# Rotary embedding on one core: unit 0's output is stored mostly from GpSimd's queue behind the loads, instead of from SyncE's beside them

## The chip, the cores and the metric

One core of a Trainium2 chip. The metric is the device time of one execution in microseconds (us). The profile's span is some 1.8 us shorter than that time.

## The reference

The input x is 8 x 8 x 1024 x 64 in float32 (16.78 MB), and the output has the same shape and type.

```python
angles = np.outer(positions * scale, freqs)          # scale = 0.5
cos, sin = np.cos(angles), np.sin(angles)
x_first, x_second = x[..., :half], x[..., half:]
out_first  = x_first * cos - x_second * sin
out_second = x_first * sin + x_second * cos
```

## The kernel before

The 64 heads are worked on in four units of 128 partitions x 8192 numbers, 4.19 MB each in float32. GpSimd's queue loads the units and casts them to float16 on the way. The first half of unit 0 comes this way too; its second half is staged in float32 through SyncE's and ScalarE's queues, in a buffer of the output pool. After a prologue that makes the tables of sines and cosines, VectorE (DVE in the profile) does four operations for each half unit. ScalarE (ACT) casts the half to float32 in an output buffer, and a DMA stores it.

```python
    xin = ctx.enter_context(tc.tile_pool(name="xin", bufs=1))
    xout = ctx.enter_context(tc.tile_pool(name="xout", bufs=3))   # staged half of unit 0, then OUT
    # ... (staged half, small tables)
    pin(nc.gpsimd.dma_start(out=Xf[0][:, :NH], in_=xv[0][:, :NH]))
    # ...
    for u in range(1, NU):
        pin(nc.gpsimd.dma_start(out=Xf[u], in_=xv[u]))
    # ... (tables of sin and cos into T)
    for u in range(NU):                       # NU = 4
        OUT = xout.tile([P, N], FP32, tag="O")        # N = 8192
        for s in range(2):
            # ... (ks, ns, Xs: the half; sin_b, cos_b: the tables, broadcast)
            pin(nc.vector.tensor_tensor(out=pr, in0=Xs, in1=sin_b, op=ALU.mult))
            pin(nc.vector.tensor_tensor(out=Xs, in0=Xs, in1=cos_b, op=ALU.mult))
            # ... (a subtraction and an addition, half as long)
            pin(nc.scalar.copy(out=OUT[:, ns], in_=Xf[u][:, ns]))
            if u in (0, NU - 1):
                pin(nc.sync.dma_start(out=ov[u][:, ns], in_=OUT[:, ns]))
        if u not in (0, NU - 1):
            pin(nc.gpsimd.dma_start(out=ov[u], in_=OUT))
```

Of the kernel before, what the change touches and what calls it, by code (L numbers as in the profile page):

```python
# [21 lines left out]
def kernel(  # L22
# [8 lines left out]
    nc = tc.nc  # L31
    pin = tc.keep_in_program_order
# [9 lines left out]
    NU = NBH // HEADS  # L42
# [2 lines left out]
    K8 = S // P  # L45
    G = P // HP
    W = K8 * half
    assert S % HP == 0 and D == 2 * half and NBH % HEADS == 0 and G * K8 == K

    fscale = float(scale)  # L50
# [2 lines left out]
    ov = out.rearrange("b h s d -> (b h s d)").rearrange("(u p n) -> u p n", p=P, n=N)  # L53
# [34 lines left out]
        out=one, in_=one, compare_op=ALU.not_equal, fill=1.0, base=0,  # L88
        pattern=[[-1, G], [-G, HP]], channel_multiplier=1,
    ))  # L90
    for u in range(1, NU):
# [9 lines left out]
        out=posf, in_=pos_i64.bitcast(I32).rearrange("p (k t) -> p k t", t=2)[:, :, 0]  # L101
# [3 lines left out]
        out=y,  # L105
# [8 lines left out]
        out=r, in0=m, scalar=_MAGIC, in1=y, op0=ALU.subtract, op1=ALU.subtract  # L114
# [5 lines left out]
        out=ra.bitcast(I32), in0=r.bitcast(I32), scalar1=0x7FFFFFFF, scalar2=None, op0=ALU.bitwise_and  # L120
# [5 lines left out]
    for g in range(0, G, 2):  # L126
        ps = spread.tile([P, 2, 2, W], FP32, tag="g")
        for i in range(2):
            nc.tensor.matmul(  # L129
                out=ps[:, i].rearrange("p t w -> p (t w)"),  # L130
# [9 lines left out]
    pin(nc.scalar.copy(out=Xf[0][:, NH:], in_=X0f[:, :NH]))  # L140


    for u in range(NU):
        OUT = xout.tile([P, N], FP32, tag="O")
        for s in range(2):
            ks = slice(s * KH, (s + 1) * KH)
            ns = slice(s * NH, (s + 1) * NH)
            Xs = X[u][:, ks]
            sin_b = T[:, 0, ks].unsqueeze(2).broadcast_to((P, KH, 2, half))
            cos_b = T[:, 1, ks].unsqueeze(2).broadcast_to((P, KH, 2, half))  # L150
            pr = tmp.tile([P, KH, 2, half], FP16, tag="pr")
            pin(nc.vector.tensor_tensor(out=pr, in0=Xs, in1=sin_b, op=ALU.mult))  # L152
            pin(nc.vector.tensor_tensor(out=Xs, in0=Xs, in1=cos_b, op=ALU.mult))  # L153
            pin(nc.vector.tensor_tensor(  # L154
                out=Xs[:, :, 0, :], in0=Xs[:, :, 0, :], in1=pr[:, :, 1, :], op=ALU.subtract
            ))
            pin(nc.vector.tensor_tensor(  # L157
                out=Xs[:, :, 1, :], in0=pr[:, :, 0, :], in1=Xs[:, :, 1, :], op=ALU.add
            ))
            pin(nc.scalar.copy(out=OUT[:, ns], in_=Xf[u][:, ns]))  # L160
            if u in (0, NU - 1):
                pin(nc.sync.dma_start(out=ov[u][:, ns], in_=OUT[:, ns]))
        if u not in (0, NU - 1):
            pin(nc.gpsimd.dma_start(out=ov[u], in_=OUT))  # L164
# [1 line left out]
_INS = ['x', 'freqs', 'positions', 'scale']  # L166
_OUTS = [((8, 8, 1024, 64), 'float32')]
# [30 lines left out]
```

## Time and profile before

| | us |
|---|---|
| time, median of 3 runs | 84.39 |
| span of the profile | 82.5 |
| engine total: shares of the DMA queues, summed, times the span | 80.0 |
| data of the last store ready | 73.2 |
| last store landed | 81.6 |

The profile gives each DMA queue's packet time as a share of the 16 engines' span. Their sum times the span is how long 16 engines need for all the bytes. By the bytes they carry, q0 in the profile is GpSimd's queue, q1 SyncE's and q10 ScalarE's. A "DMA" row cuts the span into 40 slices and gives the engines' busy share in tenths. The page's list of DMA issues of this kernel shows where bytes wait (KB are counted on the SBUF side, the last column is the median from issue to landing):

```profile
out_dram<-OUT SPq DMA_DIRECT2D x4, 2048.0 KB, 14.8
out_dram<-OUT POOLq DMA_DIRECT2D x2, 4096.0 KB, 15.3
X<-in_x_dram POOLq DMA_DIRECT2D x3, 2048.0 KB, 31.9
```

A transfer of 2.1 MB takes 14.8 us here. At the rate of the engines it would move in 4.9, so most of the time it stands in a queue or takes turns with another.

### The profile page before, as it was taken

How to read it: one execution, taken by the hardware profiler on the slowest of the kernel's cores; microseconds unless marked ns; L12 is line 12 of the kernel's file. 1: busy time of each engine (PE TensorE's matmuls, PEld its weight loads, DVE VectorE, ACT ScalarE, POOL GpSimd, SP SyncE). 2: the span in 40 equal slices, each digit the busy share in tenths (PEclk: the TensorE clock that was granted, in tenths of full speed). 3: DMA queues.
4: the chain of work that ended last, by engine and by line, in shares of the span. 5: the costliest groups of instructions: out<-in, count | busy, mean ns of one | idle time of the engine just before them, and what ended most of it. 6: DMA issues, size and time to landing. Idle time of an engine off the chain costs nothing.

```text
span 82.5 us, 179 instructions
## 1 busy us (share of the span) xinstructions
PE 7.1 (9%) x18; PEld 2.8 (3%) x18; DVE 60.3 (73%) x40; ACT 40.1 (49%) x18; POOL 4.6 (6%) x14
## 2 busy tenths in 40 slices
PE   0020999200000000000000000000000000000000
PEld 0020333000000000000000000000000000000000
DVE  0306476999999999999999999999999997000000
ACT  0603069999950790393098059219606902940000
POOL 4920000000000000000000200000200000000000
PEclk9999999985555555555555555555555555555555
DMA  2899998997996999799979999996998999799990
GB/s 48 336 319 278 290 326 187 254 246 159 230 254 127 254 262 342 270 278 350 278 191 302 270 342 421 461 524 286 508 509 350 413 508 461 302 445 429 397 485 24
DMA packets 1874, 26.22 MB, mean 318 GB/s; under 512 B 338, under 2 KB 338, under 8 KB 338
## 3 DMA queue, kind: packets, MB, share of 16 engines
q0 software_dynamic: 864, 15.73, 66.2%
q1 hardware_dynamic: 720, 9.44, 27.5%
q10 hardware_dynamic: 290, 1.06, 3.3%
HBM read 16.79 MB, written 16.78 MB: 407 GB/s over the span
## 4 chain that ended last, share of the span: by engine, by line
DVE 55%; ACT 15%; issue 6%; DMA 5%; PE 5%; DVEq 1%; ACTq 0%
DVE X L153 20%; DVE pr L152 20%; DVE X L157 9%; DVE X L154 6%; DMA freq_row<-in_freqs_dram 5%; ACT T L139 5%; ACT OUT L160 4%; PE ps L129 4%; ACT X L140 4%; DVEq L193 1%; PE cfreq L97 1%; ACT tab L122 1%; DVE r L113 1%; DVE y L104 1%; ACTq L69 0%
## 5 line engine op out<-in xcount | busy, mean ns | idle before, releaser
L160 ACT CAST OUT<-X 128x4096 f32<-128x4096 f16 x8 | 28.9, 3607 | 24.2 <-DVE X L157 24.2
L152 DVE TENSOR_TENSOR pr<-X,T 128x4096 f16<-128x4096 f16 x8 | 18.3, 2292 | 1.0 <-ACT T L139 0.7
L153 DVE TENSOR_TENSOR X<-X,T 128x4096 f16<-128x4096 f16 x8 | 18.3, 2292 | 0.3
L154 DVE TENSOR_TENSOR X<-X,pr 128x2048 f16<-128x2048 f16 x8 | 9.8, 1225 | 0.3
L157 DVE TENSOR_TENSOR X<-pr,X 128x2048 f16<-128x2048 f16 x8 | 9.7, 1218 | 0.0
L139 ACT CAST T<-ps 128x1024 f16<-128x1024 f32 x6 | 5.7, 1028 | 2.6 <-PE ps L129 2.6
L129 PE MATMUL ps<-tab,sel 128*128 128x512 f16 x16 | 6.5, 599 | 2.2 <-ACT tab L122 2.2
L164 POOL DMA_DIRECT2D out_dram<-OUT x2 | 1.1, 538 | 54.1 <-ACT OUT L160 54.1
L137 DVE CAST T<-ps 128x1024 f16<-128x1024 f32 x2 | 2.5, 1225 | 2.2 <-PE ps L129 2.2
L140 ACT CAST X<-X0f 128x4096 f16<-128x4096 f32 x1 | 3.6, 3649 | 0.0
L95 DVE COPY sel<-one 128x2048 f16<-128x2048 f16 x1 | 0.7, 693 | 2.8 <-POOL one L87 2.8
L129 PEld LDWEIGHTS <-sel 128*128 128x128 f16 x16 | 2.3, 143 | 6.1 <-issue 6.1
L117 ACT ACTIVATE tab<-r 128x256 f16<-128x256 f32 x1 | 0.4, 418 | 4.1 <-DVE r L113 4.1
L117 ACT ACT_TABLE_LOAD x1 | 1.3, 1283 | 2.1 <-issue 2.1
L92 POOL DMA_DIRECT2D X<-in_x_dram x3 | 2.0, 658 | 0.0
L100 DVE CAST posf<-pos_i 128x8 f32<-128x8 int32 x1 | 0.2, 172 | 2.3 <-DMA pos_i<-in_positions_dram 2.3
L97 PE MATMUL cfreq<-freq_row,coef 1*128 1x32 f32 x2 | 0.6, 392 | 5.6 <-DMA freq_row<-in_freqs_dram 5.6
L83 POOL DMA_DIRECT2D X<-in_x_dram x1 | 0.7, 669 | 0.8 <-POOLq L179 0.8
L97 PEld LDWEIGHTS cfreq<-freq_row,coef 1*128 1x128 f32 x2 | 0.5, 306 | 5.6 <-issue 5.6
L104 DVE TENSOR_TENSOR y<-posf,cfreq 128x256 f32<-128x256 f32 x1 | 0.4, 422 | 0.3 <-PE cfreq L97 0.3
L122 ACT ACTIVATE tab<-ra,quarter 128x256 f16<-128x256 f32 x1 | 0.5, 507 | 0.0
L113 DVE SCALAR_TENSOR_TENSOR r<-m,y 128x256 f32<-128x256 f32 x1 | 0.4, 424 | 0.0
(10 smaller groups left out, 1.9 us busy)
## 6 DMA issues: line engine op xcount, KB each, us to landing
out_dram<-OUT SPq DMA_DIRECT2D x4, 2048.0 KB, 14.8
out_dram<-OUT POOLq DMA_DIRECT2D x2, 4096.0 KB, 15.3
X<-in_x_dram POOLq DMA_DIRECT2D x3, 2048.0 KB, 31.9
X0f<-in_x_dram SPq DMA_DIRECT2D x1, 1024.0 KB, 4.8
X<-in_x_dram POOLq DMA_DIRECT2D x1, 1024.0 KB, 11.7
X0f<-in_x_dram ACTq DMA_DIRECT2D x1, 1024.0 KB, 13.2
pos_i<-in_positions_dram ACTq DMA_DIRECT2D x1, 8.0 KB, 5.0
freq_row<-in_freqs_dram ACTq DMA_DIRECT2D x1, 0.1 KB
```

The source lines that it names most:

```text
L92: pin(nc.gpsimd.dma_start(out=Xf[u], in_=xv[u]))
L97: nc.tensor.matmul(out=cfreq, lhsT=coef, rhs=freq_row, start=True, stop=True)
L117: pin(nc.scalar.activation(out=tab[:, 0], in_=r, func=AF.Sin, bias=0.0, scale=-_TWO_PI_DN))
L129: nc.tensor.matmul(out=ps[:, i].rearrange("p t w -> p (t w)"), lhsT=sel[:, g + i].rearrange("s h q -> s (h q)"), rhs=tab.rearrange("s t k ...
L137: pin(nc.vector.tensor_copy(out=dst, in_=ps))
L139: pin(nc.scalar.copy(out=dst, in_=ps))
L140: pin(nc.scalar.copy(out=Xf[0][:, NH:], in_=X0f[:, :NH]))
L152: pin(nc.vector.tensor_tensor(out=pr, in0=Xs, in1=sin_b, op=ALU.mult))
L153: pin(nc.vector.tensor_tensor(out=Xs, in0=Xs, in1=cos_b, op=ALU.mult))
L154: pin(nc.vector.tensor_tensor(out=Xs[:, :, 0, :], in0=Xs[:, :, 0, :], in1=pr[:, :, 1, :], op=ALU.subtract))
L157: pin(nc.vector.tensor_tensor(out=Xs[:, :, 1, :], in0=pr[:, :, 0, :], in1=Xs[:, :, 1, :], op=ALU.add))
L160: pin(nc.scalar.copy(out=OUT[:, ns], in_=Xf[u][:, ns]))
```

## The change

The intent: stores of unit 0, at 24 and 31 us, should not take engine time from the loads of units 2 and 3, which are still running. Only the first 1024 of 8192 columns leave early through SyncE. The rest stands in GpSimd's queue behind the loads.

```diff
+    C1 = 1024
...
             pin(nc.scalar.copy(out=OUT[:, ns], in_=Xf[u][:, ns]))
-            if u in (0, NU - 1):
+            if u == NU - 1:
                 pin(nc.sync.dma_start(out=ov[u][:, ns], in_=OUT[:, ns]))
-        if u not in (0, NU - 1):
-            pin(nc.gpsimd.dma_start(out=ov[u], in_=OUT))
+            if (u, s) == (0, 0):
+                pin(nc.sync.dma_start(out=ov[u][:, :C1], in_=OUT[:, :C1]))
+        if u < NU - 1:
+            c = 0 if u else C1
+            pin(nc.gpsimd.dma_start(out=ov[u][:, c:], in_=OUT[:, c:]))
```

## The prediction

> **What bounds the kernel now.** I began with the page's totals, because the change moves transfers and nothing else. In the slices by time and in the table of queues, the DMA row and the shares of the three queues are what to look at.
>
> ```profile
> DMA  2899998997996999799979999996998999799990
> q0 software_dynamic: 864, 15.73, 66.2%
> q1 hardware_dynamic: 720, 9.44, 27.5%
> q10 hardware_dynamic: 290, 1.06, 3.3%
> HBM read 16.79 MB, written 16.78 MB: 407 GB/s over the span
> ```
>
> The shares add to 97.0% of an 82.5 us span, 80.0 us, and the row is high from the second slice to the last but one. Except for about 1.5 us at each end there is no stretch in which the 16 DMA engines have nothing to do. (The sevens in the row are an effect of how packets of the engines fall in step; they recur where the queues hold plenty of work.) The queues' bytes sum to 26.22 MB, HBM's to 33.57: the 7.34 MB that the float32 to fp16 loads put into SBUF are counted at their fp16 size, so a load costs the engines twice the bytes shown.
>
> Next, who waits for whom. Lines of the view of waits that concern the outputs and the X tiles:
>
> ```profile
> POOL out_dram L164 <- ACT OUT L160: 54.1, 2, 40.6
> ACT OUT L160 <- DVE X L157: 24.2, 7, 3.6
> DVE pr L152 <- ACT T L139: 0.7, 1, 0.7
> ```
>
> After its first product at 13.1 us VectorE (DVE) waits for nothing worth a tenth of a microsecond; no load is waited for by anything in the main loop, and ScalarE (ACT) waits for DVE alone, never for a store to free its output buffer. The loads therefore have slack already. Their issues are at 2.7, 3.6 and 4.1 us; asked one by one, they take 19.9, 31.9 and 46.0 us to land, so X1, X2, X3 land at 22.6, 35.5 and 50.1 us, and DVE starts on them at 27.3, 41.4 and 55.5. The slack is 4.7, 5.9 and 5.4 us.
>
> Last, the tail of the timeline:
>
> ```profile
> 66.19 7.33 SPq L162 DMA_DIRECT2D out_dram<-OUT  x2
> 68.31 1.22 DVE L157 TENSOR_TENSOR X<-pr,X 128x2048 f16<-128x2048 f16 x1
> 69.56 3.61 ACT L160 CAST OUT<-X 128x4096 f32<-128x4096 f16 x1 [3.40 <-DVE X L157]
> ```
>
> The last data is ready at 73.2 us and its 2.1 MB take 8.4 us to land (81.6). At the rate below, 2.1 MB need 4.9 us and some 0.7 us to land: 2 to 3 us of the tail are other stores still queued. So there are two bounds close together: the compute chain with a bare last store, 73.2 + 5.6 = 78.8 us, and the DMA engines' total, which sets the end. The chain-of-waits view gives DVE 55% and the DMA 5%, because it follows one thread back and cannot show a full queue; the engine shares can.
>
> Does the rate depend on queue, direction or mixture? The DMA view of four stretches (in order: loads alone, 15 to 23.5 us; loads beside SyncE's stores, 30 to 48; GpSimd's stores alone, 60 to 66; SyncE's stores alone, 74 to 81), with packets, MB, share of 16 engines:
>
> ```profile
> q0 software_dynamic: 128, 1.84, 101.3%
> ...
> q0 software_dynamic: 176, 2.62, 68.6%
> q1 hardware_dynamic: 176, 2.62, 34.7%
> ...
> q0 software_dynamic: 96, 2.62, 101.2%
> ...
> q1 hardware_dynamic: 203, 2.88, 96.2%
> ```
>
> HBM bytes over engine time: loads alone 2 x 1.84/(1.013 x 8.5) = 427 GB/s; in the mixture 2 x 2.62/(0.686 x 18) = 424 for the loads and 2.62/(0.347 x 18) = 419 for the stores; GpSimd's stores 2.62/(1.012 x 6) = 431; SyncE's 2.88/(0.962 x 7) = 428. A byte costs the engines the same within 3%, whoever issued it and whatever runs beside it. That is the finding on which the prediction rests.
>
> **What the Trainium skill says.** "DMA: Bandwidth & Descriptors", section "Issuing engines are not separate DMA queues": transfers from scalar, sync and gpsimd run on the same 16 engines and interleave, and issuing from several saves issue time alone. The trace agrees (419 to 431 GB/s above). The same page, "Queues, rings and completion order": each engine takes the queues that have work in turn, a packet at a time, and a queue's descriptors in order; so a store behind the loads in GpSimd's queue starts after them. The trace agrees as far as it goes: X1, X2, X3 land in order, and in the mixture the two queues moved 176 packets each. Its section "Where 436 GB/s comes from" puts the HBM side's bound at about 358 GB/s and the fabric's at 435; this trace moves 407 over the span and 431 at best, so here the 435 is the one that fits. "SBUF — State Buffer", section "SBUF: two separate sides", warns that descriptors written by GpSimd can be held up by VectorE's two-port modes. The store issues at 45.3 and 59.4 us ran beside VectorE's tensor_tensor and took 0.54 us each, 0.3 us after ACT's end; this trace shows no such hold-up, and the added issue falls beside the same operations.
>
> **The change part by part.** No instruction of DVE, ACT or PE changes. SyncE loses two stores of 2.1 MB (at 23.75 and 30.95 us) and gains one of 128 x 1024 float32, 0.52 MB, at 23.75. GpSimd gains one store of 3.67 MB, issued at about 31.2 when ACT ends the second half of unit 0: one more issue, 0.54 us on an engine that is 6% busy. Bytes: 4.19 = 0.52 + 3.67, so the engine total stays at 80.0 us. First-order gain: zero.
>
> What moves is the order. At 24 us about 7.3 MB of loads (HBM bytes) remain; with 0.52 MB of SyncE's beside them they need 7.9/0.427 = 18.4 us, so X3 lands at about 43 instead of 50.1, and X2 at about 33 instead of 35.5. Nothing waits for that. Unit 0's rest follows, 3.67/0.43 = 8.5 us, and lands at about 51 to 52. Unit 3's output takes the same buffer (three buffers, the first used by the staged input), and ACT wants it at 62.56; the present second store lands at 30.95 + 26.4 = 57.4, so the slack grows from 5 to about 11 us. Unit 1's store (issued at 45.3) would run from 51 to 61 and land at about 61.5, before 62.2; unit 2's, issued at 59.4, follows it.
>
> Then the end. At 66.2, bytes not yet moved excluding unit 3 are the same in both kernels if no engine ran dry between: some 2 MB, of unit 2. SyncE's halves join at 66.2 and 73.2, exactly as now; the backlog at 73.2 is again about 3.3 MB, 7.7 us, plus about 0.7 to land: 81.6. Sum: 84.39 + 0.
>
> **The rivals.** (1) *The queue runs dry.* With everything in GpSimd's queue, no second queue covers the change from unit 1's store to unit 2's. At 59.4 the backlog is about 0.9 MB, 2 us, against an issue of 0.54 and perhaps 1 us of start-up (estimate): barely covered. If not, about 1 us is lost: 85.4. Against it: backlog at that moment is the same in the kernel before, where SyncE's queue has been empty since 57.4 too, and there 60 to 66 is full. (2) *A gain of 1 to 2 us:* loads undisturbed, end nearer to the 78.8 bound, 82.5 to 83.4. It needs some engine time to vanish. The only source would be a dearer mixture (419 to 424 against 427 to 431, 1 to 2% over 30 us, 0.3 to 0.6 us), within the error of my reading. (3) *A buffer wait for unit 0's late store:* it would have to land after 62.56, 11 us later than worked out; then every microsecond shifts ACT and perhaps the end. The order of the queue speaks against it. (4) *The tail shares badly:* unit 2's backlog now competes with the last halves packet by packet. All of it must land anyway, so only who finishes first changes; a skew between engines might add 0.3 us.
>
> **Range and chances.** I take 84.3: zero, less a little for the mixture. Gain of up to 0.5 and loss of up to 0.7 are both plausible, so 83.8 to 85.0. Two per cent is 1.7 us: more than rival 1 costs and about what rival 2 can give at most. Within 2%: 0.95; faster 0.03; slower 0.02.
>
> **What would show it.** Right: DMA shares summing again to about 80 us, HBM bytes unchanged, X3 landing in about 39 us from its issue, unit 0's large store in about 20 us, DVE still without waits, ACT's last copy still ending near 73.2, and the last store again taking about 8 us. Wrong: a zero or low stretch in the DMA row near 60 us (rival 1), ACT waiting for a store at 62.6 (rival 3), a last store taking under 7 us (rival 2), or engine time per MB that differs from before by over 2%.

## The result, and the profile after

The changed kernel takes 84.34 us (median of 6 runs, 84.23 to 84.38), and the kernel before 84.39 (6 runs, 84.08 to 84.67). The ratio is 0.9996, with a 95% interval of 0.9974 to 1.0017: the same.

The page of the changed kernel, the same lines as of before:

```profile
DMA  3799997996999899799699999997998999799990
q0 software_dynamic: 1008, 19.40, 76.6%
q1 hardware_dynamic: 576, 5.77, 17.1%
q10 hardware_dynamic: 290, 1.06, 3.2%
HBM read 16.79 MB, written 16.78 MB: 406 GB/s over the span
```

3.67 MB have moved from q1 to q0. The shares sum to 96.9% of 82.6 us, 80.0 us, as before. The transfers themselves did change, as the page's list of issues shows:

```profile
out_dram<-OUT POOLq DMA_DIRECT2D x2, 4096.0 KB, 15.4
X<-in_x_dram POOLq DMA_DIRECT2D x3, 2048.0 KB, 29.3
out_dram<-OUT SPq DMA_DIRECT2D x2, 2048.0 KB, 9.5
out_dram<-OUT POOLq DMA_DIRECT2D x1, 3584.0 KB, 21.3
...
out_dram<-OUT SPq DMA_DIRECT2D x1, 512.0 KB, 14.5
```

Asked one by one, X2 takes 29.3 us to land (31.9 before) and X3 40.0 (46.0 before). X3 is there 6 us earlier, and nothing uses it earlier. The view of waits of the changed kernel (us in total, times, longest) still has DVE waiting for ScalarE at the start of the main loop only, 0.7 us once and 0.2 us once, and ScalarE's copies to the output waiting for DVE alone:

```profile
ACT OUT L162 <- DVE X L159: 24.2, 7, 3.6
...
DVE pr L154 <- ACT T L140: 0.7, 1, 0.7
```

The tail of the timeline of the changed kernel (start, us, instruction), to set beside the one in the prediction:

```profile
66.26 7.34 SPq L164 DMA_DIRECT2D out_dram<-OUT  x2
...
69.64 3.60 ACT L162 CAST OUT<-X 128x4096 f32<-128x4096 f16 x1 [3.40 <-DVE X L159]
```

The last data is ready at 73.2 us and its store takes 8.4 us to land; the half before it, issued at 66.3, takes 10.6. All of this is as before.

### The profile page after: what moved, and what is told of

It reads as the page before. It is cut to its first block, busy times and chain, and to the rows that moved or that the text cites. A ratio compares the mean times of both kernels' runs of the same rounds, so it can differ in the third digit from the quotient of the medians.

```text
span 82.6 us, 179 instructions
## 1 busy us (share of the span) xinstructions
PE 6.6 (8%) x18; PEld 2.6 (3%) x18; DVE 60.3 (73%) x40; ACT 40.1 (49%) x18; POOL 5.2 (6%) x15
## 3 DMA queue, kind: packets, MB, share of 16 engines
q1 hardware_dynamic: 576, 5.77, 17.1%
## 4 chain that ended last, share of the span: by engine, by line
DVE 55%; ACT 14%; issue 6%; DMA 5%; PE 5%; DVEq 1%; ACTq 0%
DVE X L155 20%; DVE pr L154 20%; DVE X L159 9%; DVE X L156 6%; DMA freq_row<-in_freqs_dram 5%; ACT T L140 5%; ACT OUT L162 4%; PE ps L130 4%; ACT X L141 4%; DVEq L198 1%; PE cfreq L98 1%; ACT tab L123 1%; DVE r L114 1%; DVE y L105 1%; ACTq L70 0%
## 5 line engine op out<-in xcount | busy, mean ns | idle before, releaser
L154 DVE TENSOR_TENSOR pr<-X,T 128x4096 f16<-128x4096 f16 x8 | 18.3, 2292 | 1.0 <-ACT T L140 0.7
L155 DVE TENSOR_TENSOR X<-X,T 128x4096 f16<-128x4096 f16 x8 | 18.3, 2292 | 0.3
L130 PE MATMUL ps<-tab,sel 128*128 128x512 f16 x16 | 6.0, 543 | 2.5 <-ACT tab L123 2.2
L169 POOL DMA_DIRECT2D out_dram<-OUT x3 | 1.6, 536 | 53.7 <-ACT OUT L162 53.7
## 6 DMA issues: line engine op xcount, KB each, us to landing
X<-in_x_dram POOLq DMA_DIRECT2D x3, 2048.0 KB, 29.3
out_dram<-OUT POOLq DMA_DIRECT2D x1, 3584.0 KB, 21.3
out_dram<-OUT SPq DMA_DIRECT2D x1, 512.0 KB, 14.5
```

The source lines that it names most:

```text
L130: nc.tensor.matmul(out=ps[:, i].rearrange("p t w -> p (t w)"), lhsT=sel[:, g + i].rearrange("s h q -> s (h q)"), rhs=tab.rearrange("s t k ...
```

## The experiments

The theory tested, D: the total of the DMA engines sets the time, and the order of transfers is free as long as their queues never run dry. The rivals: C, the compute chain sets the time, transfers are hidden, and the change did nothing for that reason; B, two effects of the change cancel at just this size; O, order never matters. Every edit starts from the changed kernel.

**VectorE's chain shortened.** Wrong result.

```diff
-            pin(nc.vector.tensor_tensor(out=Xs, in0=Xs, in1=cos_b, op=ALU.mult))
```

> The changed kernel without the multiplication by cosine: eight VectorE operations of 2.29 us less, wrong result on purpose, the same bytes. Theory D (the total of the DMA engines sets the time, and order is free as long as their queues hold work): VectorE's chain ends some 16 to 18 us earlier, the last transfer lands at about the same 81.6 us, time 84.3 (83.6 to 84.6). Rival C (the chain of VectorE sets the time, the transfers are hidden, and that is why the change did nothing): 66 to 68 us.

Measured 84.32 us (84.26 to 84.34, 4 runs) against 84.41 of before; ratio 0.9989 (0.9965 to 1.0012). The page: DVE's busy time and the DMA row, with the chain that ended last.

```profile
DVE  0306376961999999999997999900000000000000
...
DMA  3799999997998989799899999998999899998991
...
DMA 34%; ACT 20%; DVE 6%; PE 5%; ACTq 5%; issue 2%
```

VectorE is 18.3 us less busy (42.0 against 60.3), done before 54 us instead of near 70, and the time doesn't move. C is out. The chain view now says DMA 34% and DVE 6%, where it said DVE 55% and DMA 5% before. The view's lines tell why. Of the 34%, 29% is one wait of ScalarE, for unit 0's store to free its buffer; the other 5% is the load of freqs in the prologue, which is also the whole DMA share before. In the traces of these kernels that view ends with the last copy or the issue of the last store, so what that store then spends in the queue isn't in it, and it doesn't tell the bound. ScalarE's wait in the view of waits:

```profile
ACT OUT L161 <- DMA out_dram<-OUT: 5.3, 1, 5.3
```

It shows as 5.3 us, and it cost nothing either: the DMA row stays high meanwhile.

**Bytes added.**

```diff
+    spare = consts.tile([P, 3072], FP32)
...
                 pin(nc.sync.dma_start(out=ov[u][:, :C1], in_=OUT[:, :C1]))
+                pin(nc.sync.dma_start(out=spare, in_=xv[0][:, :3072]))
```

> The changed kernel with one load more on SyncE's queue behind its small store, 128 x 3072 float32 (1.57 MB) into a tile that nobody reads. Theory D: 1.57 MB at 428 GB/s, 3.7 us more, 88.0 (87.6 to 88.4), with VectorE's chain unmoved (loads have 11 us of slack). Rival C: 84.3.

Measured 88.31 us (88.23 to 88.37) against 84.17; ratio 1.0485 (1.0452 to 1.0517), which is 4.1 us. The page's queues:

```profile
q0 software_dynamic: 1008, 19.40, 72.5%
q1 hardware_dynamic: 720, 7.34, 21.5%
q10 hardware_dynamic: 290, 1.06, 3.1%
```

The engine total rose from 80.0 to 97.1% of 86.5, 84.0 us. VectorE's busy time and waits stayed. A load that nobody reads is paid in full: D holds and C is out again. The cost was 4.0 us where 428 GB/s gave 3.7; these bytes were dearer, at 393 GB/s. No run says why.

**Bytes taken away from the middle.** Wrong result.

```diff
-        if u < NU - 1:
+        if 0 < u < NU - 1:
```

> The changed kernel without GpSimd's store of unit 0 (3.67 MB less, wrong result on purpose). At 428 GB/s that is 8.6 us of engine time. Theory D with its condition: the queues then run dry, because units 1 and 2 are issued only at 45.3 and 59.4 us; from 59.4 on 8.39 MB remain, 19.6 us plus about 1 us of start and landing, end about 80.1, time 82.9 (82.4 to 83.4), so only 1.5 of the 8.6 us. Theory D without the condition: 75.7. Rival C: 84.3.

Measured 83.49 us (83.26 to 83.62) against 84.41; ratio 0.9883 (0.9851 to 0.9915). The engine total fell to 86.9% of 81.8, 71.1 us, by 8.9, and the time by 0.9. The page shows where the rest went:

```profile
DMA  2899999998997979798960569955059799699993
```

A slice is 2.05 us. Counted from 0, the row falls to 0 in slice 21 (43 to 45 us) and in slice 28 (57 to 59 us), with fives and sixes around both. Asked microsecond by microsecond, the engines stand from 42 to 46 and from 56 to 60 us, and these 8 us are the 8.9 saved less the 0.9 gained. The first hole is between the end of the loads and unit 1's issue, the second between unit 1's end and unit 2's issue. The condition of D (the queues never dry) fails here, and what was saved turned into idle engines. The expected 82.9 was 0.6 too low and the measured time just outside its range. Unit 2's issue in this run came at 59.8 instead of 59.4, and the last store landed at 81.0 instead of 80.1: start and landing took 1.6 us where I had allowed 1.

**All of GpSimd's stores taken away.** Wrong result; it measures the other bound, the compute chain with a bare last store.

```diff
-        if u < NU - 1:
-            c = 0 if u else C1
-            pin(nc.gpsimd.dma_start(out=ov[u][:, c:], in_=OUT[:, c:]))
```

> The changed kernel without any store on GpSimd (12.06 MB less, wrong result on purpose): the second bound that the prediction put at 78.8 us of span to landing, VectorE's and ScalarE's chain with a bare last store behind it. Last data at 73.3, then 2.1 MB alone, 4.9 us, and start and landing: landing at 78.8 to 79.8, time 81.5 to 82.3. A linear reading of bytes, 12.06 MB at 428 GB/s, would give 28 us less, 56.

Measured 82.17 us (81.90 to 82.32) against 84.28; ratio 0.9736 (0.9698 to 0.9773). The page's line of the last two stores:

```profile
out_dram<-OUT SPq DMA_DIRECT2D x2, 2048.0 KB, 6.3
```

The last store takes 6.3 us to land instead of 8.4, at 79.5. The engine total is 51.7 us, 28.3 below, and 26 of them are off the path. So 2.2 us is the most that removing the stores ahead of it gave, with compute and the last store as they are. The two bounds, 84.3 us by the DMA engines (VectorE's chain shortened) and 82.2 us by compute, lie that close.

**The queue left empty.** Unit 0's rest goes behind unit 1's store; bytes and correctness as in the changed kernel.

```diff
-        if u < NU - 1:
-            c = 0 if u else C1
-            pin(nc.gpsimd.dma_start(out=ov[u][:, c:], in_=OUT[:, c:]))
+        if u == 0:
+            OUT0 = OUT
+        elif u < NU - 1:
+            pin(nc.gpsimd.dma_start(out=ov[u], in_=OUT))
+            if u == 1:
+                pin(nc.gpsimd.dma_start(out=ov[0][:, C1:], in_=OUT0[:, C1:]))
```

> The changed kernel with the store of unit 0's rest issued behind that of unit 1 in GpSimd's queue: the same bytes, but the queue is empty from the end of the loads (43 to 44 us) until unit 1 is issued (45.3). Theory D: DMA engines idle for about 2 us, ACT's copy of unit 3 waits for the buffer by about 2 us (landing about 64.7 against 62.6), and the time grows by about the idle time, 86.0 to 87.0. A rival in which order never matters (O): 84.3. Rival C: 84.3 to 86.4 by the wait of ACT alone, with no part for the idle engines.

Measured 87.75 us (87.45 to 87.84) against 84.41; ratio 1.0390 (1.0359 to 1.0421). Microsecond by microsecond, of this kernel (the last two columns are the DMA share and GB/s; the share can pass 1, as a packet's time seems to be counted where the packet starts):

```profile
41.00:42.00 1.00, 0.00 (x0) 0.00 (x0) 0.97 (x2) 0.40 (x1) 0.00 (x0) 0.50 1.23 262
42.00:43.00 1.00, 0.00 (x0) 0.00 (x0) 1.00 (x1) 1.00 (x1) 0.00 (x0) 0.50 0.02 0
43.00:44.00 1.00, 0.00 (x0) 0.00 (x0) 0.97 (x2) 1.00 (x1) 0.00 (x0) 0.50 0.00 0
44.00:45.00 1.00, 0.00 (x0) 0.00 (x0) 1.00 (x1) 1.00 (x1) 0.00 (x0) 0.50 0.00 0
45.00:46.00 1.00, 0.00 (x0) 0.00 (x0) 1.00 (x1) 0.20 (x1) 0.50 (x1) 0.50 0.00 0
46.00:47.00 1.00, 0.00 (x0) 0.00 (x0) 0.97 (x2) 0.00 (x0) 0.57 (x2) 0.50 1.26 524
```

The same view of the changed kernel holds packets again from 43 us on (its 0.00 from 42 to 43 follows a share of 2.03 in the microsecond before):

```profile
42.00:43.00 1.00, 0.00 (x0) 0.00 (x0) 1.00 (x1) 1.00 (x1) 0.00 (x0) 0.50 0.00 0
43.00:44.00 1.00, 0.00 (x0) 0.00 (x0) 0.97 (x2) 1.00 (x1) 0.00 (x0) 0.50 1.10 459
```

The engine total stays (92.6% of 86.1, 79.7 us) while the span grows by 3.5 us: the engines stood idle and never got the time back. O is out. My number was about 1 us short. I had the queue empty until unit 1's issue at 45.3, but bytes start to move about 1 us after the issue (issued at 45.5; a view of 42.3 to 46.5 has no bytes). The wait of ScalarE that I expected didn't come. Its copy of unit 3 began at 62.8 us without waiting, while unit 0's store landed only at 46.0 + 19.5 = 65.5, and the result was correct; so it must have written to another buffer than unit 0's, which the trace doesn't name. So the loss is that of the idle engines alone, and what a late landing does to ScalarE while the queue is full is shown only by the 5.3 us above.

**The split at its ends.** All of unit 0 behind the loads:

```diff
-            if (u, s) == (0, 0):
-                pin(nc.sync.dma_start(out=ov[u][:, :C1], in_=OUT[:, :C1]))
...
-            c = 0 if u else C1
+            c = 0
```

> The changed kernel with all 8192 columns of unit 0 in GpSimd's queue, SyncE storing none early. Theory D: the queue still never runs dry before the loads end, so 84.3 (84.0 to 84.6), X3 landing about 1 us earlier (39 us from its issue). Rival B (two effects cancel at this size: loads that gain by it and a late store that loses): a move of half a microsecond or more in one direction as the split goes to its end.

And all stores on SyncE, none on GpSimd:

```diff
-            if u == NU - 1:
+            if True:
                 pin(nc.sync.dma_start(out=ov[u][:, ns], in_=OUT[:, ns]))
-            if (u, s) == (0, 0):
-                pin(nc.sync.dma_start(out=ov[u][:, :C1], in_=OUT[:, :C1]))
-        if u < NU - 1:
-            c = 0 if u else C1
-            pin(nc.gpsimd.dma_start(out=ov[u][:, c:], in_=OUT[:, c:]))
```

> All stores on SyncE's queue, in halves, none on GpSimd's: the opposite end of the change. Theory D: same bytes, queue never dry, 84.3 (83.9 to 84.8). Rival B: slower or faster by half a microsecond or more, as loads are disturbed most here. X3 should land as in the kernel before, about 46 us from its issue.

Measured 84.51 (84.38 to 84.52) against 84.41, ratio 1.0009 (0.9984 to 1.0033), and 84.56 (84.38 to 84.67) against 84.17, ratio 1.0036 (1.0007 to 1.0065). X3 landed 38.9 and 45.8 us after its issue, so the loads' finish moved by 7 us between the two ends. The engine totals are 96.8% of 82.7 and 96.7% of 82.6: 80.1 and 79.9 us. The two ran on different chips, so the ratios are what to compare: 0.1 and 0.3 us slower than before, and the second interval, 0.06 to 0.55 us, excludes zero. (That edit also moves the stores of units 1 and 2.) A slope of a few tenths is therefore not excluded, and order isn't quite free at that size. A cancelling of the half microsecond that B asked for doesn't appear, though the upper end of that interval just reaches it.

**Why the small store took 14.5 us.** The 0.52 MB that SyncE still stores early surprised me. The packets of each queue in the changed kernel, from 27.3 to 37.0 us:

```profile
q0 software_dynamic: 128, 1.84, 88.8%
q1 hardware_dynamic: 128, 0.52, 14.1%
```

One packet of q1 (a row of 4 KB) moved for each packet of q0 (112 are rows of a load, 32 KB in HBM; the other 16 are under 512 bytes). With 128 rows on 16 engines that is 8 turns of 1.2 us. If a turn is a row, the count of turns doesn't depend on a row's length. Two kernels vary the length of the row, one the number of rows. The first two edit one number, `C1 = 256` and `C1 = 2048`; the third is

```diff
-                pin(nc.sync.dma_start(out=ov[u][:, :C1], in_=OUT[:, :C1]))
+                pin(nc.sync.dma_start(out=ov[u][:32, :NH], in_=OUT[:32, :NH]))
...
+        if u == 0:
+            pin(nc.gpsimd.dma_start(out=ov[u][32:, :NH], in_=OUT[32:, :NH]))
+            pin(nc.gpsimd.dma_start(out=ov[u][:, NH:], in_=OUT[:, NH:]))
```

> The early store of 256 columns in place of 1024: a quarter of the bytes (0.13 MB), the same 128 rows, 8 per DMA engine. If the engines take turns between the queues row by row, it still needs 8 turns behind a load's row of about 1.23 us each and lands in 13.5 to 14.5 us. If the share goes by bytes, about 8 us (5.5 us outside the moving, as in the changed kernel's 14.5 less 9.0, and a quarter of 9.0). The time 84.3.

> The early store of 2048 columns: twice the bytes, the same 8 rows per engine. By turns: each turn longer by the row itself alone, about 0.15 us, so 15 to 17 us to landing. By bytes: 5.5 + 18 = 23 us. The time 84.3.

> On the landing of SyncE's small store (14.5 us for 0.52 MB in the changed kernel, beside loads). Here the same 0.52 MB leave early as 32 partitions x 4096 columns in place of 128 x 1024; the rest of unit 0 goes to GpSimd in two stores. If the queues take turns by row (packet) whatever its length, the store needs 2 turns per engine in place of 8 and lands in 4 to 6 us. If they share by bytes, or the store is slow for its own sake, 10 us or more. The time: 84.3 in either case.

| early store | MB | rows per engine | issue to landing, us | time, us |
|---|---|---|---|---|
| 128 rows x 256 | 0.13 | 8 | 13.8 | 84.47 |
| 128 rows x 1024 | 0.52 | 8 | 14.5 | 84.34 |
| 128 rows x 2048 | 1.05 | 8 | 17.1 | 84.04 |
| 32 rows x 4096 | 0.52 | 2 | 9.9 | 84.66 |

Eight times the bytes in the same 128 rows take 3.3 us longer; a quarter of the rows with the same bytes takes 4.6 us less. The 256 and 2048 columns land as turns by row would have it, far from a share by bytes (8 and 23 us). The 32 rows met neither expectation, 9.9 us where turns gave 4 to 6 and bytes 10 or more, but their packets decide: 31 of the 32 moved from 27.9 to 31.1 us, two turns in 3.2 us against eight in 9.7. Turns it is. My 4 to 6 us left out the fixed part. From 24 to 27.3 us the view of the changed kernel has no packet of q1 at all, but these of q0:

```profile
q0 software_dynamic: 48, 0.79, 111.6%
```

Three rows per engine of the loads came first (the 32-row kernel has the same 48 packets from 24 to 27.9 us). At the end come another 1.3 us to landing (37.0 to 38.3) in the changed kernel and 2.7 (31.1 to 33.8) with 32 rows. None of this matters for the time, where nothing waits for that store. The ratio of the 32-row kernel to before is 1.0048 (1.0017 to 1.0079), a few tenths of a microsecond that no view explains.

**The 2048-column version again.** Two runs of it had given 84.04 us, so it and the changed kernel were run in five rounds each on one chip.

> The 2048-column version again, because two runs gave 84.04, 0.4% under the kernel before. Theory D gives no reason for it: 84.3, the ratio's interval holding 1. If the gain is real: 84.0 to 84.1 again, ratio 0.995 to 0.997.

> The changed kernel again beside it, on the same chip, for comparison: 84.3 (84.2 to 84.4), ratio 0.998 to 1.001.

Measured 84.09 (83.96 to 84.23), ratio to before 0.9979 (0.9960 to 0.9998), and 84.34 (84.26 to 84.54), ratio 1.0011 (0.9995 to 1.0027). The 0.2 to 0.3 us between the two held up, against my expectation: the slowest run of the one, 84.23, is below the fastest of the other, 84.26. The interval against before only just excludes 1. The pages' engine totals differ alike, 79.8 and 79.7 us in the two builds of the 2048 columns, 80.0 and 80.0 in the changed kernel, and 80.3 with 256 columns, though the pages' rounding alone can make 0.1 of it. So the gain may sit in D's own total, as the same bytes at a slightly lower cost; why they cost less, no run shows. It is the fastest correct version that was run, and its cause stays open.

## Why the prediction was right

- *Engine total sets the end.* Shown. Taking 18.3 us from VectorE changed the time by 0.1 us, while adding 1.57 MB changed it by 4.1. It holds as long as the queues hold work and compute, 2.2 us below, isn't reached.
- *A byte costs the same whoever issues it.* Shown at the size that matters here: engine totals of 79.7 to 80.3 us in nine kernels with the same bytes (before, changed, without cosine, all behind, all on SyncE, 32 rows, 256 and 2048 columns, queue left empty). It isn't exact, and "within 3%" was too narrow: the extra load cost 4.0 us instead of 3.7, 8% more, and the early store's 4 KB rows took 9.9% of the 14 us from 26 to 40 us for 0.52 MB, some 378 GB/s. For so few bytes that is under 0.2 us.
- *Loads have slack, so earlier loads give nothing.* Shown: X3 landed 40.0 us after its issue (predicted about 39), with time unchanged; between the ends of the split it moved by 7 us, with at most the few tenths told above.
- *Unit 0's store lands in time for its buffer.* Predicted at 51 to 52 us, measured 31.3 + 21.3 = 52.6, needed at 62.6. Unit 1's, predicted at about 61.5, landed at 45.3 + 17.0 = 62.3, no earlier than before (62.2), and the last store again took 8.4.
- *Rival 1, the queue runs dry near 60 us.* It didn't: from 60 to 66 us q0 has a share of 101.2% in both traces. But the danger is real. Where an order does leave the queue empty, it costs 3.5 us of span.
- *Rival 2, a gain of 1 to 2 us.* The bound it leaned on, 78.8 us to landing, measured 79.5 with GpSimd's stores removed: a bare store takes 6.3 us to land, not 5.6, because start and landing take 1.4 us beside the 4.9, not 0.7. The room is 2.2 us, reached only by dropping 12 MB.
- *Rival 3, a wait for a buffer.* None in the changed kernel. I found no experiment that isolates it.
- *Rival 4, the tail shares badly.* It didn't: the last two stores took 10.6 and 8.4 us in both kernels.
- *The small term.* I took 0.1 us off for a dearer mixture of loads and stores. The interval of the ratio (0.26% down to 0.17% up, about 0.2 us either way) can't show such a term, and the two ends of the split give it no support. That 84.3 met 84.34 so closely is luck at this size; zero is what was shown.
- *The sevens in the DMA row.* I put them down to packets falling in step. The record supports the step but not the link. From 15 to 23.5 us, with loads alone, the finer row alternates between nines and zeros about every microsecond while the share is 101.3%, so the engines do start their packets together. That the sevens come from this was argued only.

## What to carry to other kernels

Before reordering transfers, add up the queues' shares and multiply by the span. If that total is the span but for the ends, only fewer bytes or fuller engines help, and only down to the next bound (here 2.2 us for 12 MB less). A transfer that arrives sooner where nothing waited for it gives nothing. Do check that a new order never leaves the queues empty: with the bytes unchanged, 3.5 us came on top of the span where one did. And don't read the bound from the chain of waits alone; here it named VectorE for more than half the span while VectorE could lose 18 us without effect.

## What the Trainium skill lacked or had wrong

- "DMA: Bandwidth & Descriptors", "Queues, rings and completion order": it says that engines take turns between queues by packets of some 9 to 17 descriptors, and doesn't say what this does to a store of short rows beside long ones. Here each row counted as one packet and the turn was one row, not 9 to 17 of them: 4 KB against 32 KB of HBM reads, so 0.52 MB in 128 rows took 14.5 us to land and 0.13 MB in as many rows still 13.8.
- The same page, "Where 436 GB/s comes from": it lets the HBM side bind at about 358 GB/s for transfers between HBM and SBUF, without saying that this is for two cores that share the memory. (The note under the same page's measured table does say so.) One core alone moved 407 GB/s over the whole span and 419 to 431 in the four stretches measured, reading, writing or both.
- "Perfetto Trace Analysis", "Identifying the Most-Contended Engine": it advises against occupancy for DMA, as 16 engines make it misleading. Here the share summed over the queues and averaged over the 16 engines, times the span, was steady, 79.7 to 80.3 us in nine kernels with the same bytes, and it named the bound where the chain of waits did not. The HBM traffic over the span that the page prefers was as steady while the queues held work, 405 to 408 GB/s, and fell to 390 where a queue was left empty; the total stayed at 79.7 there, and so tells idle engines from dearer bytes.
